# Two of the four weight sums of each Strassen pair: from VectorE additions to accumulating DMAs

## The chip, the cores and the metric

The kernel runs on one core of a Trainium2 chip. The time is the device time of one execution in microseconds (us); the time before is 659.07 us, the median of 3 runs (657.64 to 660.76). All profile rows come from one other execution of the same program, which took 656.68 us with a span of 654.9 us from its first instruction to its last. Engines are named as the profile does: PE multiplies matrices, PEld loads its stationary operand, DVE is VectorE, ACT is ScalarE, POOL is GpSimd, SP is SyncE, which issues nearly all loads.

## The reference

Two layers of a decoder over 256 tokens of 1024 columns. Each layer mixes tokens by three attention groups and then runs a gated feed-forward block. The change touches only the feed-forward block:

```python
h2 = rms_norm(x, ffn_norm_g[l])
x = x + (jax.nn.silu(h2 @ w_gate[l]) * (h2 @ w_up[l])) @ w_down[l]   # D_FF = 2816, float32
```

## The kernel before

**Tiling.** The 2816 columns of the feed-forward block are cut into 11 chunks of 256. A chunk's gate and up weights stand side by side, 512 columns wide, and are loaded in two halves of the contraction ("lo" for rows 0 to 511, "hi" for rows 512 to 1023). Each half is a tile of 128 partitions x 2048 numbers (1 MB, as two DMAs of 512 KB, gate and up). The tokens make two blocks of 128.

**Three products for one.** float32 is multiplied as two rounded parts. ACT (or DVE) rounds a raw weight tile into `wh` (L240), DVE subtracts to get `wl` (L494), each in two pieces of 1024 columns, and PE forms three products, high by high, low by high and high by low (L569, L570, L571). Four pairs of `wh` and `wl` buffers exist, so the splits run at most four weight tiles ahead of PE.

**Strassen pairs.** Of the chunks, (2,3), (5,6) and (8,9) are done in pairs by Strassen's scheme in its seven-product form. For chunks i and j call the weight halves b11 = (i, lo), b12 = (j, lo), b21 = (i, hi), b22 = (j, hi). Seven products replace eight, and in exchange four sums of weight tiles are needed, each over 2048 columns in two pieces:

- T3 = b12 + b22, into a tile of its own
- T1 = b11 + b12, written over b12
- T2 = T3 + b11, written over b11 (so it must come after T1 has read b11)
- T4 = T2 + b21, written over T2, after T2 has been split

`sums_thread` (L508 to L541) makes them, all by DVE `tensor_tensor` through `add_op` (L503). Three pairs in each of two layers make six pairs, thus 24 sums, or 48 additions of 128 x 1024. The extra raw tiles for b12, b22 and T3 are `tb`, `mL` and `mH`; b11, b21 and all other weights use three raw tiles. A raw tile is loaded again when its last reader is done (`Held.used`).

**Products of a pair.** PE takes them in the order P1 (b11), P7 (T3), Q5 (T1), P6 (T2), Q3 (b22), then the down projection of the block before, then P2 (b21) and Q4 (T4). DVE combines the results from the banks (L1201 and L503 on `qr`), ACT applies silu (L1174), DVE multiplies (L1180; L1177 for a chunk that is done alone), PE transposes the product `p` (L587), and ACT and DVE split the transposed result into the moving operand `qk` of the down projection (L240, L1189).

**What sets the order.** Threads of the kernel run in a planner (`Timeline`) that is part of the program: each operation has an assumed duration, and the operation that could start first is emitted next. So each engine has one fixed order of instructions, and each engine works through its own in that order; an instruction that waits holds up all behind it on its engine. `G` gives POOL an assumed duration, `V` DVE. SP's queue holds the loads in a fixed sequence. Around the feed-forward blocks POOL does little: it forms the norm's scale, and at the end of the first layer's block it makes rope tables for the second (`table_thread`, L1329 and L1334) in a buffer that had been `tb`.

Of the kernel before, what the change touches and what calls it, by code (L numbers as in the profile page):

```python
# [12 lines left out]
OP = mybir.AluOpType  # L13
# [165 lines left out]
def hybrid_block(  # L179
# [18 lines left out]
    nc = tc.nc  # L198
    depth = w_in.shape[0]
    x_in = x_in[0]  # L200
    out = out[0]
# [26 lines left out]
    def G(ns, emit):  # L228
        return ("op", [("POOL", ns, emit)])
# [243 lines left out]
    def pieces(n):  # L473
        return [slice(c, min(c + PIECE, n)) for c in range(0, n, PIECE)]
# [25 lines left out]
    def add_op(dst, a, b, n, sub=False):  # L500

        op = OP.subtract if sub else OP.add
        return V(n, lambda: nc.vector.tensor_tensor(dst, a, b, op=op))  # L503
# [4 lines left out]
    def sums_thread(l):  # L508


        def add(u, a, b, after=None):
            for n, cs in enumerate(pieces(u["n"])):
                if after:
                    yield ("wait", after["ready"][n])
                t = yield add_op(u["held"].tile[:, cs], a[:, cs], b[:, cs], cs.stop - cs.start)
                u["raw"][n].done(t)
            return t

        def third(i, j):
            b12, b22, t3 = loads[l, "gu", j, 0], loads[l, "gu", j, 4], units[l, "T3", i]  # L520
            yield ("wait", b12["raw"])
            yield ("wait", b22["raw"])
            t3["held"].tile = yield ("get", E[l])
            t3["held"].slots = E[l]
            e = yield from add(t3, b12["held"].tile, b22["held"].tile)
            b22["held"].used(e)

        two = [b for b in BLOCKS if len(b) == 2]
        yield from third(*two[0])
        for (i, j), after in zip(two, two[1:] + [None]):  # L530
            b11, b12, b21 = loads[l, "gu", i, 0], loads[l, "gu", j, 0], loads[l, "gu", i, 4]
            t1, t2, t3, t4 = [units[l, f"T{n}", i] for n in (1, 2, 3, 4)]
            yield ("wait", b11["raw"])
            yield from add(t1, b11["held"].tile, b12["held"].tile)
            e = yield from add(t2, t3["held"].tile, b11["held"].tile, units[l, "gu", i, 0])
            t3["held"].used(e)
            if after:
                yield from third(*after)
            yield ("wait", b21["raw"])
            e = yield from add(t4, t2["held"].tile, b21["held"].tile, t2)  # L540
            b21["held"].used(e)  # L541

    def split_rank():
# [830 lines left out]
    def main():  # L1374
        for l in range(depth):
# [102 lines left out]
            for us, t in (((0, 1), 0), ((0,), 1), ((2, 3), 0), ((1,), 1), ((2, 3), 1)):  # L1478
                order = [
                    (u, k, kt, hf)  # L1480
                    for u in us for k, kt in enumerate(OUT_ORDER[u]) for hf in range(2)
                ]
                if us[0] == 2:
                    order.sort(key=lambda v: v[3])
                for u, k, kt, hf in order:
                    wt = yield from weight(l, "out", OUT_ORDER[u][0], k=k)
                    yield ("wait", mix[mixed[u]][t])
                    e = yield mm3(
                        bk[t][hf], cur["mT"], kt, toks(t), wt, k, slice(512 * hf, 512 * hf + 512),
                        u == 0 and k == 0, u == 3 and k == 1,  # L1490
                    )
                    if u == 3 and k == 1:
                        full[t][hf].done(e)
                if t == 1:
                    for u in us:
                        drop(e, l, "out", OUT_ORDER[u][0])
                if us == (1,):
                    E[l] = Slots([tile_([P, 2048], tag="tb", own=False)])
                    e_open[l].done(e)
                    tl.spawn(sums_thread(l), sums_rank)  # L1500
# [200 lines left out]
```

## Time and profile before

| | |
|---|---|
| median of the runs | 659.07 us (657.64 to 660.76, 3 runs) |
| the profiled execution | 656.68 us, span 654.9 us |
| PE busy | 636.6 us, 97% |
| DVE busy | 560.0 us, 86% |
| ACT busy | 403.5 us, 62% |
| POOL busy | 89.4 us, 14% |
| packets' share of the 16 DMA engines, queue of SP | 52.1% |

The first feed-forward block runs from about 150 to 335 us of the span, the second from about 468 to 650. A span row of a window gives the busy time of each engine in that stretch, with the number of instructions in brackets. A timeline row gives start, length, engine, line and tiles; in square brackets stands how long the engine was idle just before, and what ended that. PE's matmuls follow one another every 0.23 us (starts 0.22 to 0.23 apart where nothing waits), though a single one is shown 0.39 us long.

### The profile page before, as it was taken

The page shows a single profiled execution, that of the slowest core. Times are in us where ns is not written, and L with a number is a line of the kernel's source. Part 1 is how long each engine was busy: PE and PEld are TensorE (multiplying, and loading weights), DVE is VectorE, ACT ScalarE, POOL GpSimd, SP SyncE. Part 2 cuts the span into 40 slices and gives each one's busy share as a digit, 9 for nine tenths or more (in the row PEclk, how much of TensorE's full clock was granted, in tenths as well). Part 3 has the DMA queues.
Part 4 walks back from the last instruction along what each step waited for, and adds up shares of the span by engine and source line. Part 5 has one row for each costly group of instructions (what it writes and reads, how often), then busy time and mean ns, then how long its engine had stood idle before and what let it go on. Part 6 is the DMA issues. An engine that isn't in the chain of part 4 may idle for free.

```text
span 654.9 us, 8906 instructions
## 1 busy us (share of the span) xinstructions
PE 636.6 (97%) x3180; PEld 522.6 (80%) x3180; DVE 560.0 (86%) x948; ACT 403.5 (62%) x746; POOL 89.4 (14%) x119
## 2 busy tenths in 40 slices
PE   9999999989999999999999999999999999999997
PEld 7887787867788788887889778888877878888886
DVE  5889999557999989999578899995499998999961
ACT  6566678646755656566446666885476475575640
POOL 1507430010000000080020315301100000000000
PEclk9999999989999999999999999999999999999999
DMA  8982434507647557418647244453294576571721
GB/s 250 320 285 65 129 130 143 179 2 232 210 139 256 192 162 249 167 37 288 227 131 235 64 130 150 147 161 122 77 309 144 180 256 193 158 234 57 247 75 65
DMA packets 73777, 111.29 MB, mean 170 GB/s; under 512 B 2658, under 2 KB 54660, under 8 KB 73732
## 3 DMA queue, kind: packets, MB, share of 16 engines
q1 hardware_dynamic: 73700, 110.71, 52.1%
q8 instruction: 25, 0.41, 0.3%
q14 instruction: 20, 0.16, 0.1%
q10 hardware_dynamic: 32, 0.01, 0.0%
HBM read 109.66 MB, written 1.05 MB: 169 GB/s over the span
## 4 chain that ended last, share of the span: by engine, by line
PE 63%; DVE 25%; DMA 4%; issue 3%; POOL 2%; ACT 2%; SPq 0%; DVEq 0%; ACTq 0%; POOLq 0%
PE bank L571 18%; PE bank L569 18%; PE bank L570 18%; DVE wl L494 10%; PE bank L587 4%; DMA mH<-in_w_up_dram 2%; PE bank L1036 1%; DVE raw L503 1%; DVE qr L503 1%; PE bank L986 1%; DMA raw<-in_w_in_dram 1%; ACT wh L240 1%; DMA w<-in_diff_lambda_dram 1%; DVE w L1201 1%; POOL rq L580 1%
## 5 line engine op out<-in xcount | busy, mean ns | idle before, releaser
L494 DVE TENSOR_TENSOR wl<-raw,wh 128x1024 fp32r<-128x1024 f32 (+4 forms) x209 | 250.0, 1204 | 16.1 <-ACT wh L240 15.4
L240 ACT ACTIVATE wh<-raw 128x1024 fp32r<-128x1024 f32 (+4 forms) x208 | 210.1, 1039 | 84.8 <-PE bank L571 34.8
L569 PE MATMUL bank<-wh,hH 128*128 128x512 f32 (+3 forms) x488 | 191.8, 393 | 0.3 <-ACT hH L240 0.3
L571 PE MATMUL bank<-wh,hL 128*128 128x512 f32 (+3 forms) x488 | 185.5, 380 | 2.5 <-DVE hL L619 2.5
L570 PE MATMUL bank<-wl,hH 128*128 128x512 f32 (+3 forms) x488 | 184.8, 379 | 0.0
L571 PEld LDWEIGHTS bank<-wh,hL 128*128 128x128 f32 x488 | 91.7, 188 | 20.8 <-DVE hL L619 4.3
L569 PEld LDWEIGHTS bank<-wh,hH 128*128 128x128 f32 x488 | 92.0, 188 | 16.7 <-issue 2.0
L570 PEld LDWEIGHTS bank<-wl,hH 128*128 128x128 f32 x488 | 92.0, 188 | 14.2 <-DVE wl L494 0.6
L571 PE MATMUL bank<-wh,qk 128*128 128x512 f32 x176 | 68.8, 391 | 1.0 <-DVE qk L1189 1.0
L569 PE MATMUL bank<-wh,qk 128*128 128x512 f32 x176 | 69.4, 394 | 0.0
L570 PE MATMUL bank<-wl,qk 128*128 128x512 f32 x176 | 68.6, 390 | 0.0
L240 ACT ACTIVATE qk<-bank 128x256 fp32r<-128x256 f32 (+4 forms) x76 | 29.1, 404 | 33.3 <-PE bank L587 28.6
L571 PEld LDWEIGHTS bank<-wh,qk 128*128 128x128 f32 x176 | 33.0, 188 | 8.7 <-DVE qk L1189 1.9
L570 PEld LDWEIGHTS bank<-wl,qk 128*128 128x128 f32 x176 | 33.1, 188 | 6.5
L569 PEld LDWEIGHTS bank<-wh,qk 128*128 128x128 f32 x176 | 33.0, 188 | 6.5
L569 PE MATMUL bank<-wh,pv 128*128 128x512 f32 x96 | 37.3, 389 | 0.0
L570 PE MATMUL bank<-wl,pv 128*128 128x512 f32 x96 | 37.3, 389 | 0.0
L571 PE MATMUL bank<-wh,pv 128*128 128x512 f32 x96 | 37.3, 389 | 0.0
L587 PE MATMUL bank<-ident,p 128*128 128x128 f32 x160 | 28.2, 277 | 4.0 <-DVE qk L1189 1.9
L587 PEld LDWEIGHTS bank<-ident,p 128*128 128x128 f32 x160 | 19.8, 140 | 14.9 <-DVE qk L1189 2.4
L967 ACT ACTIVATE p<-p,small 128x128 f32<-128x128 f32 (+1 forms) x64 | 28.4, 448 | 1.1 <-DVE small L956 1.1
L569 PE MATMUL bank<-wh,mH 128*128 128x512 f32 x64 | 26.9, 421 | 1.2 <-ACT mH L242 1.2
(146 smaller groups left out, 920.6 us busy)
## 6 DMA issues: line engine op xcount, KB each, us to landing
raw<-in_w_in_dram SPq DMA_DIRECT2D x22, 1024.0 KB, 5.1
raw<-in_w_down_dram SPq DMA_DIRECT2D x22, 1024.0 KB, 5.0
raw<-in_w_gate_dram SPq DMA_DIRECT2D x32, 512.0 KB, 4.0
raw<-in_w_up_dram SPq DMA_DIRECT2D x32, 512.0 KB, 5.1
raw<-in_w_out_dram SPq DMA_DIRECT2D x8, 1024.0 KB, 4.9
raw<-in_w_in_dram SPq DMA_DIRECT2D x4, 768.0 KB, 5.3
tb<-in_w_gate_dram SPq DMA_DIRECT2D x4, 512.0 KB, 5.2
tb<-in_w_up_dram SPq DMA_DIRECT2D x4, 512.0 KB, 6.2
```

The costliest lines, as they stand in the source:

```text
L240: nc.scalar.activation(dst, src, AF.Copy)
L494: lambda: nc.vector.tensor_sub(lo[:, cs], raw[:, cs], h[:, cs].bitcast(F32)),
L503: return V(n, lambda: nc.vector.tensor_tensor(dst, a, b, op=op))
L569: nc.tensor.matmul(o, aH[:, kt, tok], wH[:, k, cols], start=start, stop=False)
L570: nc.tensor.matmul(o, aH[:, kt, tok], wL[:, k, cols], start=False, stop=False)
L571: nc.tensor.matmul(o, aL[:, kt, tok], wH[:, k, cols], start=False, stop=stop)
L580: 290 + 166 * n, lambda: nc.gpsimd.tensor_tensor(dst, dst, nhalf[:, :n], op=OP.pow)
L587: nc.tensor.transpose(o, i, ident)
L967: lambda: nc.scalar.activation(p[:, spans[t]], p[:, spans[t]], AF.Exp, bias=mn[:, t : t + 1], scale=-1.0, accum_out=se[t],),
L986: nc.tensor.matmul(two[e][:, t * P : t * P + n], qT[rows, pair, toks(t)], kT[rows, pair, :n], start=True, stop=True,)
L1036: nc.tensor.matmul(o, pT[:, toks(t)], v[0][:, cols], start=True, stop=t == 0)
L1201: 512, lambda: nc.vector.tensor_add(dst, at[name], other), bank=at[name]
```

## The change

T1 and T4 are no longer added by DVE. GpSimd issues DMAs that read one SBUF tile and add it into another in place (`accum_op`): T1 as b12 += b11, T4 as T2 += b21, each again in two pieces of 128 x 1024 (512 KB). The planner counts 1000 ns of POOL for each and takes the data as there 4000 ns after that. T2 stays on DVE, and its thread now waits until the planner's time for T1's last piece. T3 is as before.

```diff
+        def add_dma(u, b, after=None):
+            for n, cs in enumerate(pieces(u["n"])):
+                if after:
+                    yield ("wait", after["ready"][n])
+                dst = u["held"].tile[:, cs]
+                t = yield G(
+                    1000, lambda: nc.gpsimd.dma_start(out=dst, in_=b[:, cs], accum_op=OP.add)
+                )
+                u["raw"][n].done(t + 4000.0)
+            return t + 4000.0
...
             yield ("wait", b11["raw"])
-            yield from add(t1, b11["held"].tile, b12["held"].tile)
+            yield from add_dma(t1, b11["held"].tile)
+            yield ("wait", t1["raw"][-1])
             e = yield from add(t2, t3["held"].tile, b11["held"].tile, units[l, "gu", i, 0])
...
-            e = yield from add(t4, t2["held"].tile, b21["held"].tile, t2)
+            e = yield from add_dma(t4, b21["held"].tile, t2)
             b21["held"].used(e)
```

The changed kernel has 13 lines more, so a line of the kernel before from L535 on stands 13 lower in the changed one (L1189 is L1202, L1177 is L1190, L1201 is L1214, L1180 is L1193, L587 is L600). Since the planner places everything anew, the order moves on DVE, ACT and PE as well. SP's order is the same.

DVE around T1 and T2 of the first pair (tb is b12 and becomes T1, raw_15 is b11 and becomes T2, mL is T3, p_39 the product of the chunk before the pair). Before:

```order
L503 TENSOR_TENSOR tb_90_1343<-raw_15_90,tb_90_1343 128x1024
L648 TENSOR_TENSOR qk_91_1362<-qk_91_1362 128x512
L503 TENSOR_TENSOR tb_90_1343<-raw_15_90,tb_90_1343 128x1024
L652 TENSOR_TENSOR pv_94_1465<-qk_91_1362,pv_94_1465 128x512
L494 TENSOR_TENSOR wl_23_98<-raw_17_92,wh_22_97 128x1024
L1177 TENSOR_TENSOR p_39_114<-bank0_63,p_39_114 128x256
L494 TENSOR_TENSOR wl_25_100<-raw_15_90,wh_24_99 128x1024
L1189 TENSOR_TENSOR qk_95_1561<-bank7_70,qk_95_1561 128x2x128
L503 TENSOR_TENSOR raw_15_90<-mL_93_1396,raw_15_90 128x1024
```

and in the changed kernel:

```order
L1190 TENSOR_TENSOR p_39_114<-bank0_63,p_39_114 128x256
L661 TENSOR_TENSOR qk_91_1362<-qk_91_1362 128x512
L494 TENSOR_TENSOR wl_23_98<-raw_17_92,wh_22_97 128x1024
L665 TENSOR_TENSOR pv_94_1465<-qk_91_1362,pv_94_1465 128x512
L494 TENSOR_TENSOR wl_25_100<-raw_15_90,wh_24_99 128x1024
L1202 TENSOR_TENSOR qk_95_1561<-bank7_70,qk_95_1561 128x2x128
L494 TENSOR_TENSOR wl_25_100<-raw_15_90,wh_24_99 128x1024
L1202 TENSOR_TENSOR qk_95_1561<-bank2_65,qk_95_1561 128x2x128
L503 TENSOR_TENSOR raw_15_90<-mL_93_1396,raw_15_90 128x1024
```

The two additions into tb are gone, p_39's product stands where the first of them stood, and a second `wl_25` and a second L1202 have come ahead of T2's first addition, which now waits for T1's first DMA (its second addition for the second DMA).

DVE around T4 of the same pair (raw_17 is b21, raw_15 is T2 and becomes T4, mH is T3 of the next pair, the `w2` and `qr` rows combine the pair's products). Before:

```order
L494 TENSOR_TENSOR wl_21_96<-raw_17_92,wh_20_95 128x1024
L503 TENSOR_TENSOR raw_15_90<-raw_15_90,raw_17_92 128x1024
L494 TENSOR_TENSOR wl_21_96<-raw_17_92,wh_20_95 128x1024
L503 TENSOR_TENSOR raw_15_90<-raw_15_90,raw_17_92 128x1024
L1201 TENSOR_TENSOR w2_27_102<-bank7_70,w2_26_101 128x512
L494 TENSOR_TENSOR wl_23_98<-raw_15_90,wh_22_97 128x1024
L503 TENSOR_TENSOR qr_32_107<-qr_31_106,w2_27_102 128x512
L494 TENSOR_TENSOR wl_23_98<-raw_15_90,wh_22_97 128x1024
L1201 TENSOR_TENSOR w2_27_102<-bank0_63,w2_27_102 128x512
```

and in the changed kernel:

```order
L494 TENSOR_TENSOR wl_21_96<-raw_17_92,wh_20_95 128x1024
L1214 TENSOR_TENSOR w2_27_102<-bank7_70,w2_26_101 128x512
L494 TENSOR_TENSOR wl_21_96<-raw_17_92,wh_20_95 128x1024
L503 TENSOR_TENSOR qr_32_107<-qr_31_106,w2_27_102 128x512
L1214 TENSOR_TENSOR w2_27_102<-bank5_68,w2_27_102 128x512
L503 TENSOR_TENSOR qr_31_106<-qr_31_106,w2_27_102 128x512
L1214 TENSOR_TENSOR qr_32_107<-bank2_65,qr_32_107 128x512
L1193 TENSOR_TENSOR p_34_109<-qr_31_106,p_34_109 128x256
L494 TENSOR_TENSOR wl_23_98<-raw_15_90,wh_22_97 128x1024
L1193 TENSOR_TENSOR p_37_112<-qr_32_107,p_37_112 128x256
```

T4's additions are gone, the combining of the products has moved ahead of T4's split (`wl_23`), and the first product p_34 comes ahead of it too.

PE, where the pair's products p_34, p_37, p_38 and p_36 are transposed (wh_18 with hH there is the next chunk's weight). Before:

```order
L571 MATMUL bank0_63<-wh_18_93,hL_65_140 128x512
L587 MATMUL bank2_65<-ident_3_73,p_34_109 128x128 x2
L587 MATMUL bank4_67<-ident_3_73,p_37_112 128x128 x2
L587 MATMUL bank7_70<-ident_3_73,p_38_113 128x128 x2
L587 MATMUL bank2_65<-ident_3_73,p_36_111 128x128 x2
```

and in the changed kernel (wh_20 is b21, so these are the first matmuls of P2):

```order
L582 MATMUL bank7_70<-wh_20_95,hH_64_139 128x512
L583 MATMUL bank7_70<-wl_21_96,hH_64_139 128x512
L584 MATMUL bank7_70<-wh_20_95,hL_65_140 128x512
L600 MATMUL bank4_67<-ident_3_73,p_34_109 128x128 x2
L582 MATMUL bank7_70<-wh_20_95,hH_64_139 128x512
```

The four transposes no longer stand together: p_34's follow the first three matmuls of P2, p_37's come six matmuls later, p_38's and p_36's in the chunk that follows the pair.

## Rows read from the trace of the kernel before

**Rows 1.** The page, part 1: busy time and share of each engine.

```profile
PE 636.6 (97%) x3180; PEld 522.6 (80%) x3180; DVE 560.0 (86%) x948; ACT 403.5 (62%) x746; POOL 89.4 (14%) x119
```

**Rows 2.** Windows: stretch, its us, PE, PEld, DVE, ACT, POOL busy, clock, DMA, GB/s.

```profile
170.00:180.00 10.00, 8.89 (x41) 6.82 (x39) 10.00 (x13) 7.90 (x12) 0.00 (x0) 1.00 0.53 188
210.00:220.00 10.00, 9.07 (x44) 7.22 (x44) 10.00 (x18) 7.81 (x14) 0.00 (x0) 1.00 0.74 249
300.00:310.00 10.00, 9.76 (x47) 7.41 (x46) 10.00 (x16) 8.10 (x13) 0.00 (x0) 1.00 0.85 297
...
490.00:500.00 10.00, 8.93 (x40) 6.71 (x38) 10.00 (x15) 6.20 (x10) 0.00 (x0) 1.00 0.42 142
530.00:540.00 10.00, 9.03 (x45) 7.20 (x44) 9.59 (x16) 6.89 (x13) 0.00 (x0) 1.00 0.67 217
```

**Rows 3.** Timeline of PE at both waits of the first pair: start, length, what.

```profile
175.30 0.39 PE L571 MATMUL bank<-wh,hL 128*128 128x512 f32 x1
176.30 0.41 PE L587 MATMUL bank<-ident,p 128*128 128x128 f32 x2 [0.61 <-DVE p L1177]
...
176.78 0.40 PE L570 MATMUL bank<-wl,qk 128*128 128x512 f32 x1
177.67 0.50 PE L571 MATMUL bank<-wh,qk 128*128 128x512 f32 x1 [0.50 <-DVE qk L1189]
...
213.00 0.82 PE L587 MATMUL bank<-ident,p 128*128 128x128 f32 x6
214.75 0.44 PE L587 MATMUL bank<-ident,p 128*128 128x128 f32 x2 [0.93 <-DVE qk L1189]
```

**Rows 4.** The chain that ended last, ahead of those two waits: start, us, what.

```profile
172.94 1.14 DVE tb L503
...
199.75 1.14 DVE raw L503
200.88 0.60 DVE w L1201
```

**Rows 5.** Timeline of DVE around T1 and T2 of the first pair.

```profile
171.13 1.21 DVE L503 TENSOR_TENSOR tb<-raw,tb 128x1024 f32<-128x1024 f32 x1
...
172.87 1.21 DVE L503 TENSOR_TENSOR tb<-raw,tb 128x1024 f32<-128x1024 f32 x1
...
175.74 0.41 DVE L1177 TENSOR_TENSOR p<-bank,p 128x256 f32<-128x256 f32 x1
...
177.21 0.41 DVE L1189 TENSOR_TENSOR qk<-bank,qk 128x256 fp32r<-128x256 f32 x1
177.54 1.21 DVE L503 TENSOR_TENSOR raw<-mL,raw 128x1024 f32<-128x1024 f32 x1
```

**Rows 6.** Groups of DVE's additions by shape: count, busy us, mean ns.

```profile
L503 DVE TENSOR_TENSOR raw<-raw,raw 128x1024 f32<-128x1024 f32 x12 | 15.4, 1284 | 0.0
L503 DVE TENSOR_TENSOR tb<-raw,tb 128x1024 f32<-128x1024 f32 x4 | 4.9, 1213 | 0.0
```

**Rows 7.** Timeline of ACT: the split of b11 starts when b11 has landed.

```profile
170.54 2.01 ACT L240 ACTIVATE wh<-raw 128x1024 fp32r<-128x1024 f32 x2
```

**Rows 8.** The page, part 6: loads, KB each, median us from issue to landing.

```profile
raw<-in_w_down_dram SPq DMA_DIRECT2D x22, 1024.0 KB, 5.0
raw<-in_w_gate_dram SPq DMA_DIRECT2D x32, 512.0 KB, 4.0
raw<-in_w_up_dram SPq DMA_DIRECT2D x32, 512.0 KB, 5.1
```

**Rows 9.** POOL's table operations: count, ns at least, median, at most, first and last start.

```profile
L1334 POOL TENSOR_TENSOR tb<-gqk,ropes x16: 386/840/1378, 19.4 to 291.5; 128x96 f32<-128x96 f32 x16
```

**Rows 10.** Timeline of DVE: an addition beside those table operations.

```profile
282.27 1.62 DVE L503 TENSOR_TENSOR raw<-raw,raw 128x1024 f32<-128x1024 f32 x1
```

**Rows 11.** Timeline of PE: the first matmuls of P2 of the first pair.

```profile
202.12 0.39 PE L569 MATMUL bank<-wh,hH 128*128 128x512 f32 x1
202.34 0.39 PE L570 MATMUL bank<-wl,hH 128*128 128x512 f32 x1
```

**Rows 12.** Timeline of DVE: T4's second addition and the first combining of products.

```profile
199.66 1.22 DVE L503 TENSOR_TENSOR raw<-raw,raw 128x1024 f32<-128x1024 f32 x1
200.80 0.68 DVE L1201 TENSOR_TENSOR w<-bank,w 128x512 f32<-128x512 f32 x1
```

## The prediction

> **What bounds the kernel now.** I read the page first: PE is busy for 97% of the span, DVE for 86% [rows 1]. PE is therefore the engine to fill, and all that any relief elsewhere can win is the time in which PE stands still inside the two feed-forward blocks. Next come the windows of 10 us. In those blocks nearly all show PE at 10.00; among those that don't, two in the first block fall to 8.89 and 9.07 and two in the second, at the same places of the program, to 8.93 and 9.03; one more, at the last pair of the first block, shows 9.76 [rows 2]. (The windows that hold the norm ahead of each block also lose some; the change does not reach them.) DVE is full, 10.00, in four of these five and 9.59 in the fifth, at a granted clock of 1.00 throughout. So PE is short of work where DVE has too much.
>
> The timeline of PE says what ended each wait. In the first pair PE starts a matmul at 175.30 and the next, a transpose, at 176.30, freed by DVE's L1177; then 176.78 and 177.67, freed by L1189 [rows 3]. Starts usually lie 0.23 apart, as in the two matmuls of P2 [rows 11], so these two lose (1.00 - 0.23) + (0.89 - 0.23) = 1.43 us. At the end of the pair six transposes start at 213.00; at about 0.11 each they would be followed at 213.66, and the next starts at 214.75: 1.09 lost, again to L1189 [rows 3]. Last, the chain of waits: ahead of the first place it goes through T1's additions on DVE, ahead of the second through T4's [rows 4]. What the change takes from DVE is thus on the path that sets the end, if only for about 5 us in all.
>
> **What is removed.** 24 additions. Twelve are T4's, 15.4 us together, and twelve are T1's, in three groups of four, one of which is shown with 4.9 us [rows 6]: about 30 us of DVE's 560. Most of it lies beside a full PE and is worth nothing. Per pair DVE is given back 4 x 1.14 = 4.56 us [rows 4], more than the wait of 1.43 and the wait of 1.09. In the first pair L1177 for p_39 stands in the changed order where T1's first addition started, 171.13 instead of 175.74 [rows 5]; that ends the first wait, and the second, which followed from it. The two additions of T4 stood directly ahead of the combining of the products [rows 12], and 2.28 us less there is more than 1.09. Both layers show the same pattern, so the sum removed is 2 x (1.43 + 1.09) = 5.04 us. I don't count these places as clean afterwards: the last pair, where little is queued, still loses 0.24 [rows 2], and I leave that much at each of the four: 0.96 charged.
>
> **What is added: the DMAs, and a wait.** No accumulating DMA and no DMA issued by POOL is in the trace, so its cost is bounded from loads. A load of 512 KB lands 4.0 us after its issue, one of 1024 KB after 5.0 [rows 8]; so 512 KB more cost 1.0 us, and the rest, 3.0, is latency. Below: T1's two pieces as if they were one load of 1 MB, 5.0 us. Above: POOL's issue at the length of its longest small table operation, 1.4 [rows 9], then the two pieces at twice the bytes, 3.0 + 4 x 1.0, and all of it behind one load of 1 MB in flight, 5.0: 13.4 us. (The last third of such a load is in flight when T1 starts: DMA engines are 0.53 busy in that window [rows 2].) I take the middle, 9.2, near to the sum without the load in the way, 8.4.
>
> The Trainium skill, "Collectives: The Full Stack", section "The bandwidth ceiling: the fold count and why AG ≠ RS ≠ AR", holds that a reducing DMA is slower than a copying one for its two source reads, by a factor of two. No row here shows that; by it alone the pair of pieces would land after 8.4 us, by plain bytes after 6.4, and the forecast would move by less than 1 us.
>
> **What waits for them.** T2 is the place. Its first addition waits for T1's first DMA, its second for the second, and DVE is in order, so behind it stand T2, the splits of T3, T1, T2 and b22, and the combining of the products. Without T1 DVE would reach T2 at 177.54 - 2 x 1.14 for the additions gone + 1.14 + 0.33 for the split and the L1189 that now come first [rows 4, 5] = 176.73. From there to the end of p_34's product the changed order has 16 operations of 1024 columns (1.14), 5 of 512 (0.60 from one start to the next) and 4 of 256 (0.33): 22.56 us, so p_34 is ready at 199.29. Its transposes now follow P2's third matmul, which PE reaches at 202.12 - 1.43 + 3 x 0.23 = 201.4 [rows 11]. The slack is 2.1 us. So T1's first piece may land at 178.8, its second 1.47 later at 180.3; b11 is there at 170.54 [rows 7], and the second piece has 9.7 us. A further debit: while POOL worked on its tables a DVE addition took 1.62 us instead of 1.22 [rows 10, 12]. If POOL's issue does the same to two additions per pair, 0.8 of the slack is used and the limit is 8.9. At 9.2 T1 is 0.3 late, in the first pair of each layer: 0.6 charged. The two later pairs load b11 further ahead of its use and have more room, and I charge nothing there.
>
> T4 has more room still. Its first DMA can go as soon as T2's first piece is split, about 188, and Q4 comes 2.7 us after P2, at about 203.5; less 2.4 us for the two splits, there are some 13 us. A raw tile that is freed by T4 at 200.9 now is freed when its DMA has landed, sooner if that takes under 12 us: no cost. On POOL nothing waits behind T1 and T4 but the rope tables of the second layer, which are needed 80 us later. The DMAs add 12 MB to 111 MB of traffic, in windows with DMA at 0.4 to 0.9; loads are late by about the 2 us that a pair of pieces takes, and the splits that use them run up to four tiles ahead: no cost, and up to 2 us per layer if that lead is gone.
>
> **The sum.** -5.04 + 0.96 + 0.6 = -3.5 us, from 656.7 in the profiled execution to 653.2. The median of the runs stands 2.4 above that execution; with the same difference subtracted from it, 659.07 - 3.5 = 655.6 us.
>
> **Rivals.** 0.5%, or 3.3 us, is about what a measurement of this kernel can tell from no change.
>
> First, *nothing to measure*: T1 lands between 9.3 and 12.6 us after b11, so that T2's wait on DVE gives back what the additions cost. The price is one slope: beyond 8.9, each us of T1 costs 1 us in the first pair of each layer, 2 us in all. At 11 us the sum is -5.04 + 0.96 + 4.2 = +0.1, or 659.2. For it: the slack is 2 us and all bounds are estimates. Against: two thirds of the bounds lie below it. One mechanism of POOL would lead here too: its small table operations take 0.39 us at least and 1.38 at most [rows 9], the long ones beside a full DVE, and DVE is full where T1 is issued. If writing descriptors is held up likewise by 1 us per DMA, T1 lands at 11. The Trainium skill, "SBUF — State Buffer", section "SBUF: two separate sides", has a harsher form of that, a DMA issued by GpSimd starved of descriptors while VectorE runs a two-port operation; the operations around T1 are additions and subtractions of two tensors, which it does not count among these, and no run here shows either. Chance of this rival 0.33.
>
> Second, *slower*: the accumulation itself runs far below the rate of a load. The place is again T2 behind T1 in the first pair, and it decides from 12.6 us on; at the upper bound of 13.4 the sum is +4.9, or 664.0, and at 16 us +10.1, or 669.2. For it: nothing in the trace shows the rate of an addition in the DMA engines. Against: it needs more than all the doubled bytes plus a load in the way. Chance 0.22.
>
> Third, *the full gain*: T1 lands in under 8.9 us and no wait is left: 659.07 - 5.0 = 654.0. It is the near end of my forecast, not a case apart. More than that can't come from PE's idle time in these windows.
>
> **How the numbers follow.** Forecast, with its near end: 0.45; no change 0.33; slower 0.22. The same for faster, within, and slower by 0.5%. The low end is the full gain less the spread of the runs below their median, 1.4: 652.6, rounded to 652. The high end is the upper bound of the DMAs, 664. Beyond lie the worst of the slower case and little below 652, together under 2 in 10.
>
> **What would show it.** Right: no wait of PE for L1190 (the old L1177) at about 172 to 176 in the first pair, the windows that stood at 8.89 to 9.07 near 9.7, DVE at about 530 us busy. DVE's first T2 addition waiting for a DMA under 2 us. Wrong on the DMAs: DVE idle before T2's first addition for 4 us or more, PE waiting after it. Wrong on the cover: ACT or DVE waiting for T4's pieces ahead of L1174, or PE waiting for loads. Wrong on the bound: DVE relieved and PE's gaps still there, ended by other lines.

## The result and the profile after

The changed kernel takes 662.41 us (median of 7 runs, 661.01 to 668.07), the kernel before 658.43 us beside it (7 runs): a ratio of 1.008, 95% interval 1.0052 to 1.0107. A second measurement of the same two gave 1.0082 (1.0058 to 1.0107). The change makes the kernel 0.8% slower, 5 us, where 3.5 us less were forecast.

The profiled execution of the changed kernel took 661.01 us, that of before 656.68. The page first: busy time, then two of the DMA queues (packets, MB, share of 16 engines; q0 holds POOL's DMAs), then T4's issues.

```profile
PE 637.5 (97%) x3180; PEld 522.6 (79%) x3180; DVE 537.4 (82%) x924; ACT 403.9 (61%) x746; POOL 104.7 (16%) x143
...
q1 hardware_dynamic: 73700, 110.71, 51.4%
q0 software_dynamic: 3456, 12.58, 10.4%
...
raw<-raw POOLq DMA_DIRECT2D x12, 512.0 KB, 8.4
```

DVE has lost its 24 additions, 537.4 us against 560.0 [rows 1]. The windows that were short in PE before [rows 2], and one more:

```profile
170.00:180.00 10.00, 10.00 (x46) 7.96 (x45) 9.38 (x14) 7.59 (x12) 2.01 (x2) 1.00 1.07 249
180.00:190.00 10.00, 8.65 (x39) 6.86 (x39) 8.93 (x10) 6.16 (x8) 0.86 (x1) 1.00 0.63 208
210.00:220.00 10.00, 10.00 (x49) 8.22 (x48) 10.00 (x15) 7.98 (x12) 0.36 (x1) 1.00 0.98 335
300.00:310.00 10.00, 7.51 (x36) 5.77 (x35) 10.00 (x15) 7.76 (x12) 0.00 (x0) 1.00 0.91 311
490.00:500.00 10.00, 10.00 (x47) 8.23 (x46) 9.32 (x14) 7.55 (x13) 1.85 (x2) 1.00 1.02 274
530.00:540.00 10.00, 10.00 (x49) 8.24 (x48) 10.00 (x15) 7.84 (x12) 0.00 (x0) 1.00 0.97 338
```

Four of the five are full. But 300 to 310 has gone from 9.76 to 7.51, and 180 to 190, full before, is short: the waits have moved. The DMA share, 0.53 and 0.42 from 170 and from 490 us before, is now above 1 there.

**The place behind T2.** PE's timeline in the first pair, and DVE's:

```profile
180.95 0.39 PE L584 MATMUL bank<-wh,qk 128*128 128x512 f32 x1
182.69 0.44 PE L600 MATMUL bank<-ident,p 128*128 128x128 f32 x2 [1.35 <-DVE p L1190]
```

```profile
177.82 1.22 DVE L503 TENSOR_TENSOR raw<-mL,raw 128x1024 f32<-128x1024 f32 x1
178.96 0.42 DVE L1202 TENSOR_TENSOR qk<-bank,qk 128x256 fp32r<-128x256 f32 x1
181.07 1.23 DVE L503 TENSOR_TENSOR raw<-mL,raw 128x1024 f32<-128x1024 f32 x1 [1.69 <-DMA tb<-raw]
182.21 0.42 DVE L1190 TENSOR_TENSOR p<-bank,p 128x256 f32<-128x256 f32 x1
```

T2's second addition waits 1.69 us for T1's second DMA, directly behind it stands the multiplication of `p_35` (L1190), and PE waits for that: 182.69 - 180.95 - 0.23 = 1.5 us lost. The 1.43 us that went at 175 us [rows 3] came back here. In the second layer PE loses 0.3 us or less at this place, in both profiles of the changed kernel. ACT's rows show when b11 was there (its split, the first row) and when T1's second piece was (its split, the second):

```profile
171.65 2.01 ACT L240 ACTIVATE wh<-raw 128x1024 fp32r<-128x1024 f32 x2
...
181.00 1.06 ACT L240 ACTIVATE wh<-tb 128x1024 fp32r<-128x1024 f32 x1 [2.36 <-DMA tb<-raw]
```

**The place near 300 us.** PE's timeline at the end of the last pair's products, then DVE's and POOL's about 15 us ahead of it:

```profile
299.86 0.39 PE L584 MATMUL bank<-wh,hL 128*128 128x512 f32 x1
302.50 0.44 PE L600 MATMUL bank<-ident,p 128*128 128x128 f32 x2 [2.25 <-DVE p L1193]
```

```profile
284.87 4.24 DVE L494 TENSOR_TENSOR wl<-mL,wh 128x1024 fp32r<-128x1024 f32 x2 [1.34 <-ACT wh L240]
289.03 5.54 DVE L494 TENSOR_TENSOR wl<-raw,wh 128x1024 fp32r<-128x1024 f32 x3
```

```profile
283.83 0.87 POOL L526 DMA_DIRECT2D raw<-raw  x1 [0.27 <-DVE wl L494]
284.40 0.93 POOL L1342 TENSOR_TENSOR tb<-gqk,ropes 128x192 f32<-128x192 f32 x1
```

From start to start this took 0.63 us before, 0.40 more than usual; now it is 2.64, 2.41 more. The rope tables of the second layer began at 277 us before; now they begin at 284.40, behind T4's DMAs in POOL's queue. Beside them five subtractions take 4.24 + 5.54 = 9.78 us, 1.96 each, where additions beside the tables took up to 1.62 [rows 10] and 1.22 elsewhere [rows 12]. In the second profile of this kernel two of them took 6.81 us, one of the two alone 5.47 (shortest, median and longest in ns stand in the row below it):

```profile
285.09 6.81 DVE L494 TENSOR_TENSOR wl<-mL,wh 128x1024 fp32r<-128x1024 f32 x2 [1.21 <-ACT wh L240]
```

```profile
L494 DVE TENSOR_TENSOR wl<-mL,wh x2: 1411/3442/5474, 285.1 to 290.5; 128x1024 fp32r<-128x1024 f32 x2
```

**A load beside T4.** In that second profile, in the second layer's first pair, there is one more: the DMA issues from 511.0 to 513.6 us, then DVE and PE.

```profile
raw<-raw POOLq DMA_DIRECT2D x2, 512.0 KB, 8.8
tb<-in_w_up_dram SPq DMA_DIRECT2D x1, 512.0 KB, 9.3
```

```profile
520.96 1.23 DVE L503 TENSOR_TENSOR mH<-mL,tb 128x1024 f32<-128x1024 f32 x1 [4.30 <-issue]
```

```profile
527.82 0.39 PE L584 MATMUL bank<-wh,hL 128*128 128x512 f32 x1
530.37 0.44 PE L600 MATMUL bank<-ident,p 128*128 128x128 f32 x2 [2.16 <-DVE p L1193]
```

The load of the next pair's b22 lands 9.3 us after its issue, not 5.1 [rows 8], in flight with T4's DMAs; T3's addition needs it and holds DVE for 4.3 us, with the combining of products behind it; PE loses 2.3 us. (The releaser is named "issue" here; the load landed at 520.78.) In the first profile the same load took 6.3 us and PE lost 0.2: this cost differs from run to run.

**The head of the second block.** Here DVE waits for `mH`, the b22 of the first pair, to form T3; no T1 and no T4 of this layer has been formed yet.

```profile
478.32 0.40 PE L583 MATMUL bank<-wl,hH 128*128 128x512 f32 x1
481.20 0.50 PE L584 MATMUL bank<-wh,hL 128*128 128x512 f32 x1 [2.48 <-DVE hL L632]
...
482.02 0.63 PE L584 MATMUL bank<-wh,hL 128*128 128x512 f32 x1
482.45 0.63 PE L582 MATMUL bank<-wh,hH 128*128 128x512 f32 x1
```

PE waits 2.88 us from start to start, and behind it some 3 us in which matmuls start every 0.43 us instead of 0.23 (granted clock 0.70 in the window 480 to 485: the lower level, 1.2 GHz). In the profile of before the wait was 1.46:

```profile
475.52 0.40 PE L570 MATMUL bank<-wl,hH 128*128 128x512 f32 x1
476.98 0.50 PE L571 MATMUL bank<-wh,hL 128*128 128x512 f32 x1 [1.06 <-DVE hL L619]
```

The table sums this up for all profiles: how much later (+) or sooner than in the first profile of before PE came through three parts of the program, by the starts of matmuls of the same number in its sequence of 3180 (first block from the 880th to the 1640th, head of the second from the 2400th to the 2440th, second block from there to the last), and beside it the ratio over the runs. One profile is one execution; the ratio is the verdict.

| kernel | first block | head of the second | second block | ratio (95% interval) |
|---|---|---|---|---|
| before, again | -0.1 | +0.1 | +0.9 | |
| changed | +1.7 | +3.0 | -1.8 | 1.008 (1.0052 to 1.0107) |
| changed, again | +3.9 | +3.3 | +1.4 | 1.0082 (1.0058 to 1.0107) |
| `neither` | -2.8 | +2.5 | -2.9 | 0.9914 (0.9895 to 0.9932) |
| `t1_only` | -0.4 | +0.7 | -0.2 | 0.9978 (0.996 to 0.9995) |
| `t4_only` | +2.7 | +0.7 | -1.1 | 0.9995 (0.9983 to 1.0008) |
| `t4_not_last` | +0.8 | +2.9 | -0.5 | 1.0046 (1.0031 to 1.0062) |
| `no_tables` | +2.2 | +0.3 | +0.3 | 0.9991 (0.9974 to 1.0007) |
| `later_only` | +5.7 | +0.3 | -0.1 | 1.0064 (1.0041 to 1.0087) |
| `first_full` | -0.2 | 0.0 | -0.2 | 0.9987 (0.9968 to 1.0007) |
| `first_half` | -2.2 | +0.6 | -2.2 | 0.9933 (0.9915 to 0.995) |
| `t2_in_t3` | +4.3 | +0.5 | +0.3 | 1.0063 (1.0039 to 1.0088) |
| `first_late` | +4.8 | +0.7 | +1.8 | 1.0143 (1.0109 to 1.0177) |
| `first_late_t1` | -1.4 | +2.8 | -2.3 | 0.9957 (0.9936 to 0.9977) |
| `first_late_copy` | +6.2 | +3.4 | +1.1 | 1.0105 (1.0045 to 1.0166) |

### The profile page after: what moved, and what is told of

Read it like the earlier page. It is cut to its first block, busy times and chain, and to the rows that moved or that the text cites. A ratio compares the mean times of both kernels' runs of the same rounds, so it can differ in the third digit from the quotient of the medians.

```text
span 659.2 us, 8954 instructions
## 1 busy us (share of the span) xinstructions
PE 637.5 (97%) x3180; PEld 522.6 (79%) x3180; DVE 537.4 (82%) x924; ACT 403.9 (61%) x746; POOL 104.7 (16%) x143
## 4 chain that ended last, share of the span: by engine, by line
PE 67%; DVE 18%; DMA 8%; POOL 2%; issue 2%; ACT 2%; SPq 1%; DVEq 0%; POOLq 0%; ACTq 0%
PE bank L584 20%; PE bank L582 20%; PE bank L583 20%; DVE wl L494 6%; PE bank L600 4%; DMA tb<-raw 2%; DMA mH<-in_w_up_dram 2%; PE bank L1049 1%; PE bank L999 1%; DVE qr L503 1%; DMA w<-in_diff_lambda_dram 1%; DMA tb<-in_w_up_dram 1%; DMA x<-in_x_dram 1%; DVE qr L732 1%; POOL rq L593 1%
## 5 line engine op out<-in xcount | busy, mean ns | idle before, releaser
L600 PE MATMUL bank<-ident,p 128*128 128x128 f32 x160 | 29.0, 278 | 4.9 <-DVE p L1193 2.7
L600 PEld LDWEIGHTS bank<-ident,p 128*128 128x128 f32 x160 | 19.9, 140 | 17.2 <-DVE p L1193 5.3
```

Source lines behind the costliest of these rows:

```text
L600: nc.tensor.transpose(o, i, ident)
```

## The experiments

The theory: the relief of DVE is worth what was forecast, and three waits take it back and more: T2 behind T1, the tables behind T4, the load beside T4. (The head of the second block is a fourth place; what makes its wait long was not found.) All edits are to the changed kernel's `sums_thread`, unless told.

### What relief is worth, and each half alone

`neither`: T1 and T4 are not added at all.

```diff
-            yield from add_dma(t1, b11["held"].tile)
-            yield ("wait", t1["raw"][-1])
+            for ev in t1["raw"]:
+                ev.done(b11["raw"].time)
...
-            e = yield from add_dma(t4, b21["held"].tile, t2)
+            for n, ev in enumerate(t4["raw"]):
+                yield ("wait", t2["ready"][n])
+                ev.done(t2["ready"][n].time)
+            e = t2["ready"][-1].time
```

> Neither T1 nor T4 is added anywhere (T1 is then b12 itself, T4 is T2): DVE is relieved as in the change, and there is no DMA, no wait and no traffic for it. Bounds what relief of DVE is worth. Theory (waits): the 5 us of PE's waits that the prediction counted go: 653 to 654.5. Rival (relief is worth less than counted, other waits take their place): 656 to 658.

653.79 us against 658.76: 0.9914, which is 5.7 us (4.5 to 6.9). The bound of 5.04 us that the prediction read from PE's four waits holds, though this run was among those with a long wait at the head of the second block.

`t1_only` has T4's line back as `add(t4, t2["held"].tile, b21["held"].tile, t2)`, `t4_only` T1's as `add(t1, b11["held"].tile, b12["held"].tile)`, without the wait.

> T1 alone is added by DMAs; T4 is added on DVE as before. Theory (waits): in the changed kernel T1's second DMA landed 8.0 to 10.5 us after its issue, DVE stood still for 1.7 us in the first pair and 3.1 us in the third, and POOL's twelve table operations stood behind T4's DMAs. With T1 alone the wait of PE near 213 us comes back (about 1.1 us in each layer), the one near 175 us stays replaced by one near 181 us of about 1.5 us in layer 0, and the tables start at about 279 us again. Time 659 to 661, no better than before. Rival (traffic): it is the DMA traffic of the additions that makes loads late; half of the traffic is gone, so half of the loss: about 660.4, with loads late near the head of the second block too. Rival (T4 is the harm): T1 alone gains, 656 or less.

> T4 alone is added by DMAs; T1 is added on DVE as before. Theory (waits): no DVE wait for T1, the waits of PE near 175 us stay as before (1.4 us per layer), the one near 213 us goes (1.1 us per layer), and the table operations stand behind T4's DMAs and slow DVE's additions from about 284 us on, which costs up to 2 us once. Time 657 to 659. Rival (traffic): half of the loss, about 660.4. Rival (T4 is the harm): 660 or more, with PE's wait near 300 us at 2.6 us.

657.29 and 658.64 us: T1 alone gains 0.2%, T4 alone nothing, both together lose 0.8%. So the loss is no sum of two. The theory's figure held for T4 and was too high for T1; the traffic rival's half of the loss shows in neither. With T4's DMAs PE waits near 300 us (2.61 us from start to start in `t4_only`), without them hardly (0.38 in `t1_only`).

### The repeats

`before_again` and `after_again` are the two kernels unchanged.

> The kernel before, unchanged, for a second profile. Its profiled execution took 656.7 us, 2.1 us under the median of its 26 later runs (658.8). Theory (the head of the second feed-forward block varies from run to run): a typical run shows PE waiting 2.0 to 2.4 us near 475 us, as all four later kernels do, against 1.46 in that profile, and the start, up to 56 us, up to 1 us later. Rival (the variants' late loads there come from the change): 1.4 to 1.5 us again.

> The changed kernel, unchanged, for a second profile. Its profiled execution of 661.0 us lay 1.4 under its median. Theory (tables behind T4): PE's wait near 300 us is 2.0 us or more again, those near 181 us 1.2 to 2.5 us, and further waits for late T1 or late loads are in it, since the parts alone (T1 alone 1.5 us faster than before, T4 alone the same) don't add up to 3.7 us slower. Rival (two places outside the change): the blocks are as in the first profile, -0.2 us together, and the start and the head of the second block carry the whole difference.

Before, again: the head's wait is 1.49 us, so the rival is right there, and the start was 0.9 us later. Changed, again: the first theory holds; the wait near 300 us is in it, 3.34 us and the lower clock behind it (4.3 us lost between the 1440th and the 1480th matmul), and the late load above. Over all profiles the head's wait was 1.46, 1.49 and 1.42 in both of before and `first_full`, 1.8 to 2.1 in seven, 2.4 to 3.2 in `neither`, `first_late_t1`, `t4_not_last`, `first_late_copy` and both of the changed kernel, always with the lower clock behind it in these six. The load of `mH` lands 6.1 us after the first issue in both of before, 7.5 and 7.8 in both of the changed. `neither` has no DMA of POOL's at all and a long wait there too, so it needs none of the added DMAs; `t4_only` and `later_only` have the tables behind T4's DMAs and waits of 2.14 and 1.79 us, so the tables there don't bring the long wait by themselves either. What does stayed open.

### The tables behind T4

`no_tables`: in `table_thread` the second layer's twelve operations are replaced by four fills, so the tables are left out.

```diff
+        if l:
+            for t in range(NT):
+                for key in ("rc", "rs"):
+                    e = yield G(400, lambda: nc.gpsimd.memset(cur[key][:, t], 0.0))
+            done.done(e)
+            return
```

> The whole change, with the rope tables of the second layer left out (its twelve table operations are replaced by four short fills with zero). Theory (POOL's tables behind T4's DMAs slow DVE's additions): PE's wait near 300 us falls to under 0.7 us, and the time by 2 to 3.5 us, to 659 to 660.5. Rival (T1 of the last pair lands late, and that alone makes DVE late there): the wait stays at 1.5 us or more, 661.5 to 662.5.

657.79 us: 0.9991 instead of 1.008. PE at the place near 300 us, and DVE ahead of it:

```profile
303.15 0.39 PE L584 MATMUL bank<-wh,hL 128*128 128x512 f32 x1
303.38 0.38 PE L600 MATMUL bank<-ident,p 128*128 128x128 f32 x2
```

```profile
288.15 2.36 DVE L494 TENSOR_TENSOR wl<-mL,wh 128x1024 fp32r<-128x1024 f32 x2 [1.30 <-ACT wh L240]
290.43 2.36 DVE L494 TENSOR_TENSOR wl<-raw,wh 128x1024 fp32r<-128x1024 f32 x2
```

```profile
287.70 1.84 POOL L1340 MEMSET tb<- 128x384 f32 x4
```

No wait, and 1.18 us a subtraction; the first two ran beside the fills, POOL's row, the second of them in part. T1 lands as late as in the changed kernel in this pair (DVE waits 3.17 us for it), so a late T1 alone costs nothing there. Behind T4's DMAs the tables thus cost the 2.0 and 4.3 us that PE lost at the place in the two profiles of the changed kernel. Between the two ratios lie 0.9%, some 6 us, more than expected. The rest of that is not shown to be the tables': this profile also has no long wait at the head, where the changed kernel was 3.0 and 3.3 us late. (Its +2.2 in the first block is another wait, 4.1 us at 181 us: T1's first DMA took 7.7 us in this execution and not 5.0.)

`t4_not_last` and `later_only` choose by pair:

```diff
-            e = yield from add_dma(t4, b21["held"].tile, t2)
+            how = (add_dma, ()) if after else (add, (t2["held"].tile,))
+            e = yield from how[0](t4, *how[1], b21["held"].tile, t2)
```

> The whole change, except that T4 of the last pair of each layer is added on DVE: no T4 DMA stands ahead of POOL's table operations. Theory (tables behind T4): PE's wait near 300 us falls from 2.6 us to under 1 us, and the time falls by about 2 us from 662.4 to 660.5. Rival (DVE is late there because T1 of that pair lands late, 3.1 us of DVE's wait): the wait near 300 us stays at 2 us or more and the time at 662.

660.71 us, 1.0046: the tables start at 277.87 us again, and the wait near 300 us falls from 2.6 to 1.75, not under 1. (`after` is the next pair, which the last one hasn't.) Beside tables in their old place a T1 that lands late still costs: part of the rival holds. In `t1_only`, with the tables in that place too, T1's second DMA landed 8.3 us after its issue and not 10.5, and PE lost next to nothing. DVE's wait for it, in `t4_not_last` and in `t1_only`:

```profile
275.35 1.23 DVE L503 TENSOR_TENSOR raw<-tb,raw 128x1024 f32<-128x1024 f32 x1 [3.23 <-DMA mH<-raw]
```

```profile
273.68 1.23 DVE L503 TENSOR_TENSOR raw<-tb,raw 128x1024 f32<-128x1024 f32 x1 [1.08 <-DMA mH<-raw]
```

So tables in their old place and a T1 that lands late each cost PE little alone, and cost it 1.75 - 0.23 = 1.5 us together.

`later_only` has `(i, j) != two[0]` for `after` there, and the same choice for T1.

> The complement: DMAs for T1 and T4 in the second and third pair of each layer only, the first pair on DVE. Theory (the later pairs bring nothing and cost): PE's waits of the first pair stay, 1.4 and 1.1 us per layer, and the wait near 300 us in layer 0 is 2 to 4 us: 660 to 662.5, as slow as the whole change or nearly. Rival (the harm is in the first pair): 657 to 658.5.

662.11 us, 1.0064: DMAs in the second and third pair bring nothing and cost as much as the whole change. Its window holds the dearest form of the wait, 2.88 us idle and then the lower clock (0.66), 5.4 us lost between the 1440th and the 1480th matmul:

```profile
300.00:310.00 10.00, 7.99 (x25) 6.38 (x26) 8.18 (x11) 7.09 (x11) 0.00 (x0) 0.66 0.95 329
```

### T2 behind T1

`first_half` has DMAs only in the first pair, for T1's first half and for T4; `first_full` for both halves of T1.

```diff
+            if (i, j) == two[0]:
+                e = yield from add_dma(t1, b11["held"].tile, n0=1)
+                t = yield add_op(t1["held"].tile[:, PIECE:], t1["held"].tile[:, PIECE:], b11["held"].tile[:, PIECE:], PIECE)
+                t1["raw"][1].done(t)
+                yield ("wait", t1["raw"][0])
+            else:
+                yield from add(t1, b11["held"].tile, b12["held"].tile)
```

> DMAs only in the first pair of each layer, where PE's waits were: the first half of T1 and both halves of T4; the second half of T1 and all of the other two pairs on DVE. Theory (waits): T1's first half lands 5 us after its issue, ahead of T2, and the tables are not held up. PE's wait near 213 us goes (1.1 us per layer) and most of the one near 175 us (1.4 us per layer): 3 to 5 us under before, 654 to 656. Rival (traffic): 5/24 of the DMAs' bytes and no gain, 658 to 659.5.

> Like the version with DMAs in the first pair of each layer only, but with both halves of T1 by DMA: differs from it by T1's second DMA alone, which lands 8.0 us after its issue in the first pair. Theory (waits): DVE stands 1.7 us ahead of T2's second addition and PE 1.3 to 1.6 us ahead of L1190's product for p_35 behind it, in layer 0 and up to as much in layer 1: 1.5 to 3 us above that version's 652.9, so 654.4 to 656. Rival (two pieces or one is no matter): 652.5 to 653.5.

(`n0` ends `add_dma` after one piece.) 652.89 us, 0.9933 (0.9915 to 0.995), below the time expected, faster than both kernels and nearly as fast as `neither`; and 657.47, 0.9987. The one DMA between them costs 3.6 us by the ratios, more than expected, 2 us in each block by the table. DVE's T2 in `first_half`, then in `first_full`:

```profile
178.58 1.21 DVE L503 TENSOR_TENSOR raw<-mL,raw 128x1024 f32<-128x1024 f32 x1
```

```profile
180.24 1.23 DVE L503 TENSOR_TENSOR raw<-mL,raw 128x1024 f32<-128x1024 f32 x1 [1.78 <-DMA tb<-raw]
```

`t2_in_t3` writes T2 over T3 instead of b11, so that T2 need not wait for T1's reads (the units' `held`, T2's arguments; T3's next addition moves behind T4).

```diff
-                unit((l, "T3", i), 2048, 512, Held(2), None)
+                unit((l, "T3", i), 2048, 512, hold := Held(3), None)
...
-                unit((l, "T2", i), 2048, 512, b11["held"], None)
+                unit((l, "T2", i), 2048, 512, hold, None)
```

> The whole change, but T2 is written into T3's tile instead of b11's, so that its additions need not wait until T1's DMAs have read b11; T3's next addition moves behind T4. Theory (waits): DVE no longer stands still ahead of T2, PE's wait near 181 us (1.5 us in layer 0) goes and the one near 300 us shrinks, by up to 1.5 us: 658.5 to 660, against 662.4 of the changed kernel. Rival (traffic): the DMAs and their bytes are the same, so the time stays: 661.5 to 663.

662.51 us, 1.0063: no better, the rival's figure. The wait at 181 us is gone, but loads beside T4 land 9 us after their issue, ACT waits 4.69 us for one, and PE 3.9 us at 203 us. That brought the third part of the theory.

### The load beside T4

`first_late` is `first_full` with a later finish told to the planner.

```diff
-                u["raw"][n].done(t + 4000.0)
-            return t + 4000.0
+                u["raw"][n].done(t + 4000.0 + 4000.0 * n)
+            return t + 8000.0
```

> DMAs for both halves of T1 and T4 in the first pair of each layer only, as in the version that took 657.5 us, but the planner is told a later finish for T1's second DMA and T4's (8000 ns behind its issue instead of 4000). On DVE the multiplication of p_35, T3's splits and one more L1202 now stand ahead of T2's additions, which wait for T1's reads as before. Theory (PE lost time since p_35's multiplication stood behind a waiting T2): PE's wait near 181 us falls from 1.9 us to under 0.5 us, in both layers, and the time to 653 to 655. Rival (T1's bytes or its lateness itself cost, wherever T2 stands): 656.5 to 658.

666.00 us, 1.0143: the forecast failed, its first half came true. PE loses nothing at 181 us (from the 920th to the 940th matmul it falls 0.2 us behind, in `first_full` 1.8). But in the new order the next pair's two loads start 1.2 us apart, at 183.83 and 185.01 (2.3 in the changed kernel), and T4's DMAs at 186.37 find more of the second, the next b22, still to come. Its issue to landing, DVE's wait for it, and PE's:

```profile
mL<-in_w_up_dram SPq DMA_DIRECT2D x1, 512.0 KB, 10.8
```

```profile
196.35 1.23 DVE L503 TENSOR_TENSOR mH<-tb,mL 128x1024 f32<-128x1024 f32 x1 [4.11 <-DMA mL<-in_w_up_dram]
```

```profile
200.78 0.39 PE L588 MATMUL bank<-wh,qk 128*128 128x512 f32 x1
204.49 0.69 PE L604 MATMUL bank<-ident,p 128*128 128x128 f32 x2 [3.32 <-DVE p L1197]
```

`first_late_t1` adds T4 on DVE; `first_late_copy` keeps T4's DMAs but lets them copy b21 over T2 (no `accum_op`).

> As the version of 666.0 us (first pair only, later finish told to the planner), but T4 is added on DVE: T1's two DMAs alone are left, in the first pair of each layer. Theory (T4's DMAs delay the load of the next pair's b22, and T3's addition that waits for it holds DVE): that load lands about 5 us after its issue instead of 10.8, DVE's wait of 4.1 us ahead of T3's addition goes, PE's wait near 201 us (3.7 us) goes; the one near 213 us for T4's additions (1.1 us per layer) is back: 655 to 657. Rival (the new order of the loads or of T2 is what costs): 662 or more.

> As the version of 666.0 us, but T4's two DMAs copy b21 over T2 instead of adding it (T4 is then b21): same number, size, order and waits. Theory (the addition itself is slow in the DMA engines): the DMAs land some 2 us sooner, the load of b22 is 2 to 4 us less late, and the time falls by 2 us per layer or more, to 658 to 662. Rival (any transfer of these bytes there delays the load as much): 665 to 667.

655.17 us, 0.9957 (0.9936 to 0.9977): without T4's DMAs the same order gains. The load and DVE's wait:

```profile
mL<-in_w_up_dram SPq DMA_DIRECT2D x1, 512.0 KB, 6.9
```

```profile
192.44 1.23 DVE L503 TENSOR_TENSOR mH<-tb,mL 128x1024 f32<-128x1024 f32 x1 [0.21 <-DMA mL<-in_w_up_dram]
```

So T1 by DMA gives 2.8 us (1.5 to 4.2), its two waits of 1.43, if the order leaves it time; the 1.9% between this and `first_late` are T4's DMAs in the way of loads. With the copy 665.38 us, 1.0105, in four runs from 659.56 to 668.39: the load lands after 10.7 us just so, and the rival holds by the median and by the load; it is the transfer that is in the way, not the addition.

## Why the prediction was wrong

**What bounds the kernel: right.** PE's waits in the first pairs are worth 5 us; `neither` and `first_half` show it, and the windows at 170, 210, 490 and 530 us are full.

**T1's landing: right in sum, by luck.** Forecast 9.2 us after b11, measured 180.97 - 171.65 = 9.3 (ACT starts b11's split at 171.65). But 9.2 was the middle of two bounds more than 8 us apart, and the parts were off: at 1.0 us for 512 KB, or 2.0 for twice the bytes, the pieces should land 1 to 2 us apart, and they landed at 177.19 and 180.97, 3.8 apart.

**The slack at T2: wrong.** The step took the end of `p_34`'s product at 201 us as what T2 must not delay, and found 8.9 to 9.7 us of room. The next thing on DVE behind T2 is `p_35`'s multiplication, which PE reads at 181 us. DVE was ready for T2's second addition at 181.07 - 1.69 = 179.38, so the room was 7.7 us, and 1.5 us were lost in the first pair of the first layer instead of 0.3. `first_half`, without T1's second DMA, loses nothing there.

**T4 on POOL: wrong, and the dearest step.** "On POOL nothing waits behind T1 and T4 but the rope tables of the second layer, which are needed 80 us later": true of when they are needed, but their cost lies in when they run. The prediction counted what POOL's work does to DVE for the issue of DMAs, and not for the tables that the DMAs move. The Trainium skill, "SBUF — State Buffer", section "SBUF: two separate sides", says that a VectorE operation with two SBUF inputs and a GpSimd operation that reads SBUF take turns at one pair of ports, each holding it for its whole length. The trace agrees in that subtractions beside the tables take 1.96 us on average and one once 5.47, and beside fills, which read nothing, 1.18; how the two engines take turns no row shows. The prediction had quoted only the page's words on two-port operations.

**T4 and the loads: wrong.** "loads are late by about the 2 us that a pair of pieces takes, and the splits that use them run up to four tiles ahead: no cost, and up to 2 us per layer if that lead is gone." The load that counts is read by T3's addition, which stands on DVE ahead of the combining of products, and in the second profile it was late by 4.2 us (9.3 against 5.1). PE lost 2.3 us by it there and 0.2 in the first profile. `first_late` and `first_late_t1` show the mechanism: 10.8 us with T4's DMAs in flight, 6.9 without.

**The head of the second block: in no step.** The changed kernel's two profiles are 3.0 and 3.3 us late there against the first of before, about as much as the tables took. No step of the sum covers it; as `neither` has it too, the added DMAs are not needed for it. Its cause is open, and with it that of a part of the 5 us.

**The rivals.** "Slower" came true, by none of its own mechanism: T1 landed 3 us ahead of the 12.6 us from which it was to decide. The range of 652 to 664 us holds the median, but by luck: its high end stood for a T1 that lands 13.4 us after b11, and it landed after 9.3. The factor of two for a reducing DMA, which no row bore out before, is there now (below).

## What to carry to other kernels

When work moves to another queue, follow the work that it pushes back there, and cost it where it will then run, not where it is needed. Slack behind a new wait ends at the first instruction behind it that a full engine reads, so read the order from the waiting instruction on, one row at a time. DMAs that relieve an engine pay only where that engine was waited for: in the first pair of each layer, and kept clear of loads that are due.

## What the runs showed of the hardware

- An accumulating DMA between SBUF tiles costs the DMA engines about twice a copy. The queue's shares, for T1 alone (`first_late_t1`), with T4 added (`first_late`) and with T4 copied (`first_late_copy`):

```profile
q0 software_dynamic: 576, 2.10, 1.9%
```

```profile
q0 software_dynamic: 1152, 4.19, 3.5%
```

```profile
q0 software_dynamic: 1152, 4.19, 2.6%
```

  T4's 2.1 MB take 3.5 - 1.9 = 1.6% as additions and 2.6 - 1.9 = 0.7% as copies, in the same places. The Trainium skill, "Collectives: The Full Stack", section "The bandwidth ceiling: the fold count and why AG ≠ RS ≠ AR", gives about two between ReduceScatter and AllGather, for the two source reads of an addition; these DMAs within one core show the same factor.
- A load issued 1 us ahead of two POOL DMAs of 512 KB can land as late as the first of them: at 196.22 and 196.04 us in `first_late`, at 520.78 and 520.53 in the changed kernel's second profile. It need not: in the first profile the same load landed at 515.50, the first of the two DMAs at 517.85.
- One VectorE subtraction of two SBUF tiles took 5.47 us, and not some 1.2, while POOL ran its small table operations one behind the other (changed kernel, second profile, from 285.09 us on). In the first profile the five subtractions at that place took 1.4 to 2.3 us each; the sum is nearly the same, 10.5 and 9.8 us.
- Behind six waits of PE of 2.4 us and more at the head of the second block matmuls started every 0.43 us for some 3 us (granted clock 0.70 from 480 to 485 us in the changed kernel, so in part at 1.2 GHz). Near 300 us they did so behind 2.61 us in `t4_only`, but not behind 2.64 us in the changed kernel, nor behind 2.94 us in `t2_in_t3` at 526 us. The length of the wait alone doesn't tell the cases apart.
